# Two re-placings in a hybrid attention layer: one value chunk's casts, and the post norm's half sums

## The chip, the cores and the metric

The kernel runs on one core of one Trainium2 chip. The metric is the device time of one execution in microseconds (us); smaller is better. The engines are called as the profile calls them: PE (TensorE) multiplies matrices, PEld is its weight load, DVE (VectorE) and ACT (ScalarE) do elementwise work, POOL (GpSimd) and SP (SyncE) issue DMAs. Each engine takes its own instructions strictly in the order in which they stand in its queue.

## The reference, cut to what matters

One layer over 512 latent tokens of width 1024 (x) and 256 context tokens (ctx), in float32:

```python
sh, sc, gt = _modulation(c, w_mod, b_mod)                 # gt: the gain of the post norm
h  = _rmsnorm(x, pre_g) * (1 + sc) + sh                   # hc alike from ctx
parts = _split_in(h @ w_in)                               # ten parts of 1024 columns
q, k, v = rope(heads(parts[4])), rope(heads(parts[5])), heads(parts[6])
k_c, v_c = split(hc @ w_in[:, K_OFF:V_END])
attn = _neighbourhood_attention(q, k, v, k_c, v_c, rpb)   # one softmax over window and context
y_a = (silu(z_a) * b_gate * dwconv3(c_gate * x_in)) @ w_out_conv
y_b = (silu(z_b) * attn) @ w_out_attn
y = (sigmoid(g_a) * y_a + sigmoid(g_b) * y_b) @ w_o
x = x + gt * _rmsnorm(y, post_g)
```

The change touches two pieces of this: the projection to v (and v_c) for the second group of heads, and the 1024 values of `gt`, which are a matrix-vector product of silu(c) with a third of `w_mod`.

## The kernel before, in words

Every float32 operand of a matmul is split into a rounded part H and a rest L (`split`, L66 to 76): ACT casts H (L68), DVE subtracts it (L71), and three matmuls (H·H, H·L, L·H) stand for one.

**Weights** come in chunks of 256 columns, each as four loads of 256 KB into a ring of six slots (`Chunk`, L97, on SP's queue). A plain chunk (`split`, L100) makes two casts of 128x4x256 and two subtractions of the same shape. A paired chunk (`first`, `second`) makes sums of its quarters in place in the ring (L112 to 129) and casts of 128x512, and `pair` (L304 to 327) then needs seven products (L299) in place of eight; between them ACT and DVE combine the partial sums (L310, L313, L315, L321 on ACT, L316, L324, L327 on DVE). The list `order` (L246 to 250) says in which order chunks come, and `paired` (L243) which are paired. `Chunks.load` issues the loads of the next chunk; in the attention stage the chunk's casts (`ready`) are put into the list `behind`, which is run at the end of the score block (L875).

**The attention stage** runs 64 score blocks (8 pairs of heads, 2 heads, 4 blocks of 128 tokens), written two blocks ahead. A block's bias comes by L715; its scores are L723 or L732 on PE, L739 on DVE (bias and row maximum), L746 or L750 on ACT (exponential with sum). After two blocks follow the reciprocal (L751, DVE), the scaling (L753, ACT), eight transposes (L760, PE) and the split of the result into TH (L68) and TL (L71); after four the gather L779. Into these blocks `plan` (L228) puts projection work: `keys_queries` (queries and keys of a pair; L206 and L211 project the context's keys, L217 and L218 add two halves, L628 and L629 rotate) and `values(g)` (L187 and L192 for each of six groups of tokens, g being a group of two pairs of heads). The place of this case is the end of `keys_queries(2)` and the start of `values(1)`, whose chunk is the first plain value chunk in the attention stage.

**The merge stage** (L967 to 1003) runs j = 0 to 7. Each j has two units (i = 0, 1) of 24 matmuls (L174 to 176), each followed by a gate update on DVE (L973), and the sum m of the two (L980). For j < 4 it also projects the gates of j + 4 by `merge_gates` (a `pair` with 7 x 12 matmuls L299). The new gate tile G[j + 4] lies in the buffer of G[j], so the first copy into it, L310, waits for L980 of the same j.

**The post norm's gains** are computed beside it: `gain_half` (L955) fetches half a row block of `w_mod` (128x512, 256 KB, L959, tile `wg`, three buffers) and reduces it against silu(c) on DVE (L960). Sixteen halves make the gains; L986 to 988 finish them, L995 copies and L996 transposes them in j = 4.

The order within an engine is the program's order only in part: a scheduler moves an instruction ahead where it expects it to be ready, unless `tc.keep_in_program_order` holds the instruction in its place on its engine. In the kernel before the scheduler puts all sixteen halves into j = 0 and j = 1, though the program has four in each j from 0 to 3.

Of the kernel before, what the change touches and what calls it, by code (L numbers as in the profile page):

```python
# [9 lines left out]
F32 = mybir.dt.float32  # L10
F32R = mybir.dt.float32r
AF = mybir.ActivationFunctionType
ALU = mybir.AluOpType
AX = mybir.AxisListType

P = 128
D = 1024
KT = 8
S = 512
# [4 lines left out]
PG, QG, BM, CW, CB = 0, 8, 16, 40, 64  # L24
# [3 lines left out]
def layer(ctx: ExitStack, tc, xp, ctxt, ctxT, cc, wmod, small, wfirst, win, wout, wo, rel, tab, out):  # L28
    nc = tc.nc
# [4 lines left out]
    cv = ctx.enter_context(tc.tile_pool(name="cv", bufs=2))  # L34
# [13 lines left out]
    sp = const.tile([P, 72], F32, name="sp")  # L48
# [5 lines left out]
    gains = const.tile([P, KT], F32, name="gains")  # L54
# [33 lines left out]
    class Chunk:  # L88
# [8 lines left out]
                    nc.sync.dma_start(ring[:, at + o], src[:, 2 * i + o])  # L97
                self.raws.append(ring[:, at:at + 2].rearrange("p u (k c) -> p u k c", k=4))

        def split(self):  # L100
            t = [wtile([P, 4, 2, 256]) for _ in range(2)]
            for x, raw in zip(t, self.raws):
                H, L = (x[:, :, y].rearrange("p k (u c) -> p k u c", u=2) for y in range(2))
                split(H, L, raw.rearrange("p u k c -> p k u c"))
            k = range(KT)
            return tuple([t[i // 4][:, i % 4, y] for i in k] for y in range(2)) + ([t[i // 4][:, i % 4] for i in k],)

# [28 lines left out]
    behind = None  # L136

    class Chunks:
# [5 lines left out]
        def load(self, n):  # L144
            if n < len(self.srcs) and n not in self.ahead and n not in self.raw:
                self.raw[n] = Chunk(self.srcs[n][0])
                if behind is None:
                    self.ready(n)
                else:
                    behind.append(lambda: self.ready(n))  # L150

        def ready(self, n):
            if n in self.raw:
                c, kind = self.raw.pop(n), self.srcs[n][1]
                self.ahead[n] = c.first(kind == "qk") if kind else c.split()

        def __call__(self):
            self.load(self.n)
# [82 lines left out]
        "cx": lambda j: win[2 * j], "bz": lambda j: win[2 * j + 1],  # L241
    }
    def paired(n, i):  # L243
        return n == "g" or n == "qk" and i in (2, 3, 4, 6) or n == "zb" and i < 3 or n in ("cx", "bz") and i > 3

    order = [(win[i], False) for i in range(8)] + [(qk(0), False), (vz(0, 0), False)]  # L246
    order += [(where[n](i), n if paired(n, i) else False) for f in plan for n, i in f] + [(vz(3, 1), paired("zb", 3))]
# [138 lines left out]
    with ExitStack() as p0:  # L386
# [17 lines left out]
        cols = {}  # L404
# [435 lines left out]
    for p in range(NPAIR):  # L840
        f = []
# [8 lines left out]
    blocks = [(p, h, b) for p in range(NPAIR) for h in range(2) for b in range(4)]  # L850
    pts = {n: scores(*blocks[n]) for n in range(2)}
    T = None
    behind = []
    done = 0
    for i, (p, h, b) in enumerate(blocks):
        slot = i % 8
        if slot == 0:
            items = chain(*(g for g, _ in fill[p]))
            total, done = sum(n for _, n in fill[p]), 0
        upto = -(-total * (slot + 1) // 8)  # L860
        while done < upto:
            step(items)
            done += 1
        if T is not None and b == 0:
            gather(*T)
        if i + 2 < len(blocks):
            pts[i + 2] = scores(*blocks[i + 2])
        if b == 0:
            TH = aw.tile([P, 4, 4, P], F32R, name="TH", bufs=1)
            TL = aw.tile([P, 4, 4, P], F32R, name="TL", bufs=1)  # L870
            T = p, h, TH, TL

        if b % 2:
            turn2([pts.pop(i - 1), pts.pop(i)], b - 1, TH, TL)
        for f in behind:  # L875
            f()
        behind = []
    behind = None
    last = gate2(3)
    next(last)  # L880
# [72 lines left out]
    cond = bp.tile([P, D], F32, name="cond", tag="gpost")  # L953
    nc.sync.dma_start(cond, csc.broadcast_to([P, D]))

    def gain_half(k, i):
        t = cv.tile([P, S], F32, name="wg", tag="tc", bufs=3)
        cols = slice(i * S, (i + 1) * S)
        nc.sync.dma_start(t, wmod[16 + k][:, cols])  # L959
        nc.vector.tensor_tensor_reduce(  # L960
            out=t, in0=t, in1=cond[:, cols], scale=1.0,
            scalar=sp[:, BM + 16 + k:BM + 17 + k] if i == 0 else bsc1[:, k:k + 1],
            op0=ALU.mult, op1=ALU.add, accum_out=(bsc1 if i == 0 else gains)[:, k:k + 1],
        )

    for j in range(KT):
        w = chunk()  # L967
        g = [G[j][:, i] for i in range(2)]
        if j in (4, 6):
            raws[j // 2] = G[j]  # L970
        m2 = raws[j // 2][:, j % 2]
        for i in range(2):
            nc.vector.scalar_tensor_tensor(  # L973
                out=g[i], in0=g[i], scalar=1.0, in1=unit(w, i, ua[i]), op0=ALU.add, op1=ALU.mult
            )
            if j == 7 and i == 0:
                A2 = [bp.tile([P, 2, S], F32R, name=f"A2{k}", tag=f"us{k}") for k in range(4)]
                for k in range(3):
                    split(A2[k][:, 0], A2[k][:, 1], raws[2 + k // 2][:, k % 2])
        nc.vector.tensor_add(m2, g[0], g[1])  # L980
        if j < 4:
            for n, _ in enumerate(merge_gates(j + 4)):
                for i in range(2):
                    gain_half(2 * j + n, i)
        if j == 4:
            nc.vector.tensor_mul(gains, gains, sp[:, QG:QG + KT])  # L986
            nc.vector.tensor_scalar(out=gains[:, 0:4], in0=gains[:, 0:4], scalar1=0.5, scalar2=None, op0=ALU.mult)
            nc.vector.tensor_scalar(out=gains[:, 4:8], in0=gains[:, 4:8], scalar1=-0.5, scalar2=None, op0=ALU.mult)
            gpost = bp.tile([P, D], F32, name="gpost", tag="gpost")
            for i in range(2):  # L990
                gb = cv.tile([P, S], F32, name="ta")
                ps = pj()
                for k in range(4):
                    n = 4 * i + k
                    nc.vector.tensor_copy(gb[:, k * P:(k + 1) * P], gains[:, n:n + 1].broadcast_to([P, P]))  # L995
                    nc.tensor.transpose(ps[:, k * P:(k + 1) * P], gb[:, k * P:(k + 1) * P], ident)  # L996
                nc.scalar.copy(gpost[:, i * S:(i + 1) * S], ps)
        if j == 4:
            A11, S3 = operand("A11", hp, ("u2", "u3")), operand("S3", hp, ("a2", "a3"))
            for q in range(2):  # L1000
                split(A11[q][:, 0], A11[q][:, 1], raws[q][:, :, h0])
                x = cv.tile([P, S], F32, name="tb").rearrange("p (k c) -> p k c", k=2)
                nc.vector.tensor_sub(x, raws[q][:, :, h0], raws[q][:, :, h1])
                split(S3[q][:, 0], S3[q][:, 1], x)
            B11, B12 = quarter("B11", hp, ("s0", "s1")), quarter("B12", hp, ("u0", "u1"))
            B22, B21, T2, T3 = (quarter(n, hp, (f"h{2 * i}", f"h{2 * i + 1}")) for i, n in enumerate(("B22", "B21", "T2", "T3")))
            for t, i in ((B11, (0, 0)), (B12, (0, 1)), (B22, (1, 1)), (B21, (1, 0))):
                load_block(t, *i)
        if j == 5:
            sums1(0)  # L1010
        if j == 6:
            nc.scalar.activation(const.tile([P, 1], F32, name="dummy2"), G[7][:, 1, :1], AF.Sqrt, bias=eps, scale=0.0)
            wB11 = moving(B11)
            total(B11, B11, B12)
            T1 = B11
            total(T2, T1, B22)
            total(T3, B12, B22)
            T4 = B12
            total(T4, T2, B21)
# [208 lines left out]
```

## Time and profile before

| | us |
|---|---|
| median of 3 runs (lowest, highest) | 706.83 (706.29, 706.86) |
| the profiled execution's own time | 707.08 |
| its span, first to last instruction | 705.3 |
| PE busy | 692.5 (98%) |
| DVE busy | 603.1 (86%) |
| ACT busy | 444.4 (63%) |
| granted TensorE clock, mean | 0.999 |

The profile is one execution; its own time is 0.25 us over the median, and 1.8 us of it lie outside the span. A timeline row gives start, duration, engine, line, operation, tiles (out<-in) and how many instructions are drawn together; in brackets stands how long the engine was idle before and what released it. Instructions overlap in their engine's pipeline, so the step from one start to the next is shorter than a duration. PE's ends are modelled, so that its idle time is read best from starts.

### The profile page before, as it was taken

How to read it: one execution, taken by the hardware profiler on the slowest of the kernel's cores; microseconds unless marked ns; L12 is line 12 of the kernel's file. 1: busy time of each engine (PE TensorE's matmuls, PEld its weight loads, DVE VectorE, ACT ScalarE, POOL GpSimd, SP SyncE). 2: the span in 40 equal slices, each digit the busy share in tenths (PEclk: the TensorE clock that was granted, in tenths of full speed). 3: DMA queues.
4: the chain of work that ended last, by engine and by line, in shares of the span. 5: the costliest groups of instructions: out<-in, count | busy, mean ns of one | idle time of the engine just before them, and what ended most of it. 6: DMA issues, size and time to landing. Idle time of an engine off the chain costs nothing.

```text
span 705.3 us, 11954 instructions
## 1 busy us (share of the span) xinstructions
PE 692.5 (98%) x4304; PEld 621.6 (88%) x4304; DVE 603.1 (86%) x1170; ACT 444.4 (63%) x895; POOL 66.7 (9%) x110
## 2 busy tenths in 40 slices
PE   7999999999999999999999999999999999999996
PEld 5888888889979999898999989999898889988885
DVE  7999998669897999878998797999799896665996
ACT  7668543558677687675875757788683434442563
POOL 0000003131040310402103113000000000000000
PEclk9999999999999999999999999999999999999999
DMA  8996845454352473453635436334464643660013
GB/s 353 406 346 197 307 167 134 111 113 131 120 135 75 117 192 121 106 149 77 169 119 128 118 104 158 100 117 138 146 216 158 201 145 111 202 246 31 31 60 120
DMA packets 51727, 108.84 MB, mean 154 GB/s; under 512 B 6610, under 2 KB 6866, under 8 KB 51668
## 3 DMA queue, kind: packets, MB, share of 16 engines
q1 hardware_dynamic: 43202, 92.73, 38.6%
q0 software_dynamic: 8320, 15.21, 11.0%
q8 instruction: 34, 0.56, 0.3%
q14 instruction: 25, 0.20, 0.1%
q10 hardware_dynamic: 146, 0.14, 0.1%
HBM read 87.60 MB, written 5.25 MB: 132 GB/s over the span
## 4 chain that ended last, share of the span: by engine, by line
PE 79%; DVE 11%; DMA 6%; ACT 3%; issue 2%; SPq 0%; ACTq 0%; POOL 0%; DVEq 0%
PE ps L299 23%; PE ps L174 8%; PE ps L176 8%; PE ps L175 8%; PE ps L187 6%; PE ps L1026 5%; DVE w L71 4%; PE ps L779 3%; PE ps L192 3%; PE ps L760 3%; DMA ring<-in_win 3%; PE ps L723 3%; PE ps L457 2%; PE ps L463 2%; PE ps L460 2%; PE ps L206 2%
## 5 line engine op out<-in xcount | busy, mean ns | idle before, releaser
L71 DVE TENSOR_TENSOR w<-ring,w 128x512 fp32r<-128x512 f32 (+1 forms) x209 | 163.1, 796 | 31.8 <-ACT w L68 30.9
L68 ACT CAST w<-ring 128x512 fp32r<-128x512 f32 (+1 forms) x209 | 142.1, 711 | 76.5 <-PE ps L176 20.9
L299 PE MATMUL ps<-S,w 128*128 128x256 f32 x1104 | 140.6, 283 | 1.4 <-ACT g L310 1.4
L299 PEld LDWEIGHTS ps<-S,w 128*128 128x128 f32 x1104 | 135.9, 192 | 1.9 <-ACT g L310 1.6
L299 PE MATMUL ps<-h,w 128*128 128x256 f32 x828 | 108.0, 284 | 0.0
L299 PEld LDWEIGHTS ps<-h,w 128*128 128x128 f32 x828 | 103.3, 191 | 2.2 <-DVE g L316 0.2
L174 PE MATMUL ps<-h,w 128*128 128x512 f32 x160 | 62.6, 391 | 0.0
L175 PE MATMUL ps<-h,w 128*128 128x512 f32 x160 | 62.5, 390 | 0.0
L176 PE MATMUL ps<-h,w 128*128 128x512 f32 x160 | 62.1, 389 | 0.0
L631 POOL DMA_DIRECT2D tc<-tb x32 | 28.6, 1048 | 291.5 <-DVE tc L629 173.1
L753 ACT ACTIVATE pt<-pt,z 128x512 f32<-128x512 f32 x64 | 43.0, 723 | 7.7 <-DVE z L751 7.6
L71 DVE TENSOR_TENSOR TL<-ps,TH 128x512 fp32r<-128x512 f32 x64 | 42.5, 681 | 0.7 <-ACT TH L68 0.3
L68 ACT CAST TH<-ps 128x512 fp32r<-128x512 f32 x64 | 35.8, 587 | 10.9 <-PE ps L760 10.9
L739 DVE CUSTOM_DVE_ANT_1 ps<-ps,bt 128x512 f32<-128x512 f32 x56 | 38.7, 691 | 4.2 <-PE ps L723 4.1
L176 PEld LDWEIGHTS ps<-h,w 128*128 128x128 f32 x160 | 30.0, 188 | 6.4
L175 PEld LDWEIGHTS ps<-h,w 128*128 128x128 f32 x160 | 30.1, 188 | 6.2
L174 PEld LDWEIGHTS ps<-h,w 128*128 128x128 f32 x160 | 30.0, 188 | 6.1
L760 PE MATMUL ps<-ident,pt 128*128 128x128 f32 x256 | 33.4, 273 | 0.6 <-ACT pt L753 0.6
L187 PE MATMUL ps<-w,h 128*128 128x512 f32 x128 | 32.3, 394 | 0.0
L760 PEld LDWEIGHTS ps<-ident,pt 128*128 128x128 f32 x256 | 29.2, 140 | 3.0 <-ACT pt L753 1.2
L746 ACT ACTIVATE pt<-ps,m 128x512 f32<-128x512 f32 x32 | 22.1, 689 | 14.6 <-DVE m L739 14.1
L779 PE MATMUL ps<-TH,V 128*128 128x256 f32 (+1 forms) x96 | 28.4, 318 | 0.0
(251 smaller groups left out, 1393.2 us busy)
## 6 DMA issues: line engine op xcount, KB each, us to landing
ring<-in_win SPq DMA_DIRECT2D x148, 256.0 KB, 3.4
wm<-in_wmod SPq DMA_DIRECT2D x26, 512.0 KB, 7.5
ring<-in_wout SPq DMA_DIRECT2D x32, 256.0 KB, 3.6
bt<-in_rel SPq DMA_DIRECT2D x16, 256.0 KB, 2.9
tc<-tb POOLq DMA_DIRECT2D x32, 128.0 KB, 2.9
wg<-in_wmod SPq DMA_DIRECT2D x16, 256.0 KB, 3.7
B<-in_wo SPq DMA_DIRECT2D x8, 512.0 KB, 6.5
fraw<-in_wfirst SPq DMA_DIRECT2D x8, 384.0 KB, 8.4
```

The lines of the kernel that those rows point to most:

```text
L68: cast = nc.scalar.copy(H, src)
L71: nc.vector.tensor_sub(L, src, H.bitcast(F32))
L174: nc.tensor.matmul(ps, lhsT=H[k][:, cs], rhs=mH[k], start=k == 0, stop=False)
L175: nc.tensor.matmul(ps, lhsT=H[k][:, cs], rhs=mL[k], start=False, stop=False)
L176: nc.tensor.matmul(ps, lhsT=L[k][:, cs], rhs=mH[k], start=False, stop=k == KT - 1)
L187: nc.tensor.matmul(ps, lhsT=mH[k][:, ts], rhs=both[k].rearrange("p a c -> p (a c)"), start=k == 0, stop=False, skip_group_check=True,)
L299: nc.tensor.matmul(ps, lhsT=w[:, x, k], rhs=act[y][k], start=start and k + o == 0, stop=k == 3 and o == 2, skip_group_check=True,)
L739: nc.vector.tensor_tensor_reduce(out=s3, in0=s3, in1=bt[:, e::4 - e][:, 0:2], scale=-1.0, scalar=3.0e38, op0=ALU.add, op1=ALU.min, accum_o ...
L753: nc.scalar.mul(x, x, z[:, i:i + 1])
L760: nc.tensor.transpose(tp[:, c], pt[:, c * P:(c + 1) * P], ident)
L779: nc.tensor.matmul(o3[:, dst], lhsT=V[p][:, kt, h], rhs=src(t), start=n == 0 and t is TH, stop=n == len(work) - 1 and t is TL,)
L1026: nc.tensor.matmul(out, lhsT=a(x, k, ts), rhs=w[y][k // 2][:, k % 2, cols], start=start and k + o == 0, stop=k == 3 and o == 2, skip_group ...
```

## The change

Two edits. In the first, `paired` marks the value chunk ("v", 1) with the kind "v". It is still split as a plain chunk, but its two casts are held in program order on ACT, and `behind` is now two lists, so that this chunk's casts are written one score block later than others'. In the second, the fetch of a half is a function of its own: three are fetched ahead of the loop, and each reduction is followed by the fetch three further on. The reductions are held in program order on DVE, one after each gate update and one after each of the two units of `merge_gates`, so four in each j from 0 to 3.

```diff
-        def split(self):
+        def split(self, pinned=False):
...
-                split(H, L, raw.rearrange("p u k c -> p k u c"))
+                split(H, L, raw.rearrange("p u k c -> p k u c"), pinned=pinned)
...
-                    behind.append(lambda: self.ready(n))
+                    behind[self.srcs[n][1] == "v"].append(lambda: self.ready(n))
...
-                self.ahead[n] = c.first(kind == "qk") if kind else c.split()
+                self.ahead[n] = c.first(kind == "qk") if kind and kind != "v" else c.split(kind == "v")
...
-        return n == "g" or n == "qk" and i in (2, 3, 4, 6) or n == "zb" and i < 3 or n in ("cx", "bz") and i > 3
+        return n == "g" or n == "v" and i == 1 or n == "qk" and i in (2, 3, 4, 6) or n == "zb" and i < 3 or n in ("cx", "bz") and i > 3
...
-    behind = []
+    behind = [], []
...
-        for f in behind:
+        for f in behind[0]:
             f()
-        behind = []
+        behind = [behind[1], []]
...
-    def gain_half(k, i):
-        t = cv.tile([P, S], F32, name="wg", tag="tc", bufs=3)
-        cols = slice(i * S, (i + 1) * S)
-        nc.sync.dma_start(t, wmod[16 + k][:, cols])
-        nc.vector.tensor_tensor_reduce(
+    halves, fetched = [(k, slice(i * S, (i + 1) * S)) for k in range(KT) for i in range(2)], []
+
+    def fetch_half():
+        if len(fetched) < len(halves):
+            k, cols = halves[len(fetched)]
+            t = cv.tile([P, S], F32, name="wg", tag="tc", bufs=3)
+            nc.sync.dma_start(t, wmod[16 + k][:, cols])
+            fetched.append(t)
...
+    def gain_half():
+        n = turned[0]
+        turned[0] += 1
+        (k, cols), t = halves[n], fetched[n]
+        tc.keep_in_program_order(nc.vector.tensor_tensor_reduce(
             out=t, in0=t, in1=cond[:, cols], scale=1.0,
...
+        ))
+        fetch_half()
+
+    for _ in range(3):
+        fetch_half()
...
+            if j < 4:
+                gain_half()
...
         nc.vector.tensor_add(m2, g[0], g[1])
         if j < 4:
-            for n, _ in enumerate(merge_gates(j + 4)):
-                for i in range(2):
-                    gain_half(2 * j + n, i)
+            for _ in merge_gates(j + 4):
+                gain_half()
```

Below the first edit, lines keep their numbers up to L955; behind it L959 becomes L962, L960 becomes L971, L973 becomes L988, L980 becomes L997, L986 to 988 become L1002 to 1004, L995 and L996 become L1011 and L1012, L1003 becomes L1019.

The order of ACT's queue around the value chunk, before. The chunk's two casts are w_1995 and w_1996; tc_1907 (L321) belongs to the keys of pair 2, ps_1985 and ps_2046 are two score blocks, and TH_1993 takes the transposes of the two blocks ahead of these.

```order
L68 CAST w_1896<-ring_105 128x512
L68 CAST w_1995<-ring_105 128x4x256
L784 COPY ta_1981<-ps_1968 64x512
L68 CAST w_1996<-ring_105 128x4x256
L746 ACTIVATE pt_1990,z_1991<-ps_1985,m_1988 128x512
L321 COPY tc_1907<-ps_1909 128x256
L68 CAST w_2235<-ring_105 128x512 x2
L68 CAST TH_1993<-ps_2058 128x512
L68 CAST TH_1993<-ps_2059 128x512
L750 ACTIVATE pt_2053,z_1991<-ps_2046,m_2051 128x512
L753 ACTIVATE pt_1990<-pt_1990,z_1991 128x512
L753 ACTIVATE pt_2053<-pt_2053,z_1991 128x512
```

The same stretch of the changed kernel, where the chunk's casts are w_2066 and w_2067:

```order
L68 CAST w_1896<-ring_105 128x512
L784 COPY ta_1981<-ps_1968 64x512
L746 ACTIVATE pt_1990,z_1991<-ps_1985,m_1988 128x512
L321 COPY tc_1907<-ps_1909 128x256
L68 CAST TH_1993<-ps_2052 128x512
L68 CAST TH_1993<-ps_2053 128x512
L68 CAST w_2066<-ring_105 128x4x256
L750 ACTIVATE pt_2047,z_1991<-ps_2040,m_2045 128x512
L68 CAST w_2067<-ring_105 128x4x256
L217 COPY ta_2101<-ps_2084 128x256
L753 ACTIVATE pt_1990<-pt_1990,z_1991 128x512
L753 ACTIVATE pt_2047<-pt_2047,z_1991 128x512
```

The exponential L746, the copy L321 and the TH casts now stand ahead of both casts of the chunk, and the first casts of the chunk after it (w_2235) have left this stretch.

PE's queue a little later in the same stage, as a difference: L760 are the transposes of the next two score blocks, L187 the first matmuls of `values(1)`.

```order
 L723 MATMUL ps<-ks,qd 128x512
 L723 MATMUL ps<-ks,qe 128x512
-L760 MATMUL ps<-ident,pt 128x128 x8
 L187 MATMUL ps<-w,h_82 128x512
 L187 MATMUL ps<-w,h_83 128x512
 L187 MATMUL ps<-w,h_84 128x512
+L760 MATMUL ps<-ident,pt 128x128 x8
 L187 MATMUL ps<-w,h_85 128x512
 L187 MATMUL ps<-w,h_86 128x512
```

Three matmuls of the value projection now stand ahead of those transposes.

DVE's queue in j = 1 of the merge stage, before: from the first half behind the first gate update to the sum m (L980) and the half behind it. Each ISA row with an input is one half's reduction, the row below it the reading of its result; g1 is the gate tile, w_6592 and w_6593 are operands of the gates of j = 5.

```order
L960 ISA wg_7061,bsc1_115<-wg_7061,cond_6320,sp_72 128x512
L960 ISA bsc1_115 128x1
L960 ISA wg_7108,bsc1_115<-wg_7108,cond_6320,sp_72 128x512
L960 ISA bsc1_115 128x1
L71 TENSOR_TENSOR w_6592<-ring_105,w_6592 128x512 x2
L960 ISA wg_7064,gains_81<-wg_7064,cond_6320,bsc1_115 128x512
L960 ISA gains_81 128x1
L973 SCALAR_TENSOR_TENSOR g1_5756<-g1_5756,ps_6564 128x512
L71 TENSOR_TENSOR w_6593<-ring_105,w_6593 128x512
L980 TENSOR_TENSOR m0_6318<-g1_5756 128x512
L960 ISA wg_7111,gains_81<-wg_7111,cond_6320,bsc1_115 128x512
```

And in the changed kernel, from the first gate update of j = 1:

```order
L988 SCALAR_TENSOR_TENSOR g1_5756<-g1_5756,ps_6544 128x512
L971 ISA wg_6402,bsc1_115<-wg_6402,cond_6320,sp_72 128x512
L971 ISA bsc1_115 128x1
L71 TENSOR_TENSOR w_6604<-ring_105,w_6604 128x512 x2
L988 SCALAR_TENSOR_TENSOR g1_5756<-g1_5756,ps_6573 128x512
L971 ISA wg_6480,gains_81<-wg_6480,cond_6320,bsc1_115 128x512
L971 ISA gains_81 128x1
L997 TENSOR_TENSOR m0_6318<-g1_5756 128x512
L71 TENSOR_TENSOR w_6605<-ring_105,w_6605 128x512
L1019 TENSOR_TENSOR tb_7209<-m0_6318 128x512
L316 TENSOR_TENSOR g5_6603<-g5_6603,ps_6613 128x256
```

Between the two gate updates one half stands where three stood, and one stands between the second update and the sum m, where none stood. L316, on DVE, needs the copy L310 and stands behind m in both kernels.

More of the change, by code (lines that the diff above doesn't have):

```diff
@@ L954, in layer @@
     nc.sync.dma_start(cond, csc.broadcast_to([P, D]))
-    def gain_half(k, i):
-        t = cv.tile([P, S], F32, name="wg", tag="tc", bufs=3)
-        cols = slice(i * S, (i + 1) * S)
-        nc.sync.dma_start(t, wmod[16 + k][:, cols])
-        nc.vector.tensor_tensor_reduce(
-            out=t, in0=t, in1=cond[:, cols], scale=1.0,
-            scalar=sp[:, BM + 16 + k:BM + 17 + k] if i == 0 else bsc1[:, k:k + 1],
-            op0=ALU.mult, op1=ALU.add, accum_out=(bsc1 if i == 0 else gains)[:, k:k + 1],
-        )
+    halves, fetched = [(k, slice(i * S, (i + 1) * S)) for k in range(KT) for i in range(2)], []
[5 more added lines that the diff above has]
+            fetched.append(t)
+    turned = [0]
+    def gain_half():
[3 more added lines that the diff above has]
+        tc.keep_in_program_order(nc.vector.tensor_tensor_reduce(
+            out=t, in0=t, in1=cond[:, cols], scale=1.0,
+            scalar=bsc1[:, k:k + 1] if n % 2 else sp[:, BM + 16 + k:BM + 17 + k],
+            op0=ALU.mult, op1=ALU.add, accum_out=(gains if n % 2 else bsc1)[:, k:k + 1],
+        ))
+        fetch_half()
+    for _ in range(3):
+        fetch_half()
     for j in range(KT):
```

## The prediction

> **What bounds the kernel now.** I read what PE waited for first, since PE is busy for 98% of the span. Its longest waits in the whole run (line; total us, times, longest):
>
> ```profile
> PE ps L507 <- ACT crow L479: 3.7, 1, 3.7
> PE ps L299 <- ACT g L310: 1.4, 1, 1.4
> PE ps L206 <- ACT tc L321: 0.7, 1, 0.7
> PE ps L760 <- ACT pt L753: 0.6, 1, 0.6
> ```
>
> The first is the start-up, which the change doesn't touch. The second lies in the merge stage, the third and fourth in the value stage, and these are the change's two places. The table by stage (length; busy us of PE, PEld, DVE, ACT, POOL; clock) shows both places and stretches without a wait:
>
> ```profile
> 188.00:204.00 16.00, 14.76 (x98) 12.85 (x97) 13.51 (x30) 11.32 (x26) 3.53 (x4) 1.00 0.55 154
> 204.00:222.00 18.00, 18.00 (x110) 15.98 (x109) 13.66 (x36) 12.09 (x32) 4.66 (x9) 1.00 0.47 113
> 240.00:266.00 26.00, 26.00 (x210) 25.39 (x209) 25.77 (x55) 21.64 (x48) 7.38 (x13) 1.00 0.69 176
> 552.00:573.00 21.00, 19.56 (x120) 17.47 (x119) 18.81 (x47) 7.51 (x12) 0.00 (x0) 1.00 0.53 177
> 573.00:594.00 21.00, 21.00 (x135) 19.10 (x134) 13.61 (x21) 8.57 (x14) 0.00 (x0) 1.00 0.37 121
> ```
>
> In rows 1 and 4 PE is idle; in the others it is busy for the whole stretch. So nearly the whole kernel is a queue of matmuls, and time saved in rows 1 and 4 reaches the end if no later stretch takes it back. PE's starts tell how long each wait is. First an undisturbed group of transposes:
>
> ```profile
> 173.15 1.03 PE L760 MATMUL ps<-ident,pt 128*128 128x128 f32 x8
> 173.94 1.31 PE L299 MATMUL ps<-h,w 128*128 128x256 f32 x9
> ```
>
> Eight of them take 0.79 from start to next start. In the value stage:
>
> ```profile
> 193.04 1.03 PE L760 MATMUL ps<-ident,pt 128*128 128x128 f32 x8
> 194.75 2.11 PE L206 MATMUL ps<-hc,w 128*128 128x512 f32 x8 [0.67 <-ACT tc L321]
> ...
> 198.11 0.39 PE L723 MATMUL ps<-ks,qd 128*128 128x512 f32 x1
> 198.34 0.40 PE L723 MATMUL ps<-ks,qe 128*128 128x512 f32 x1
> 199.31 1.27 PE L760 MATMUL ps<-ident,pt 128*128 128x128 f32 x8 [0.57 <-ACT pt L753]
> 200.34 2.09 PE L187 MATMUL ps<-w,h 128*128 128x512 f32 x8
> ```
>
> L206 could start at 193.04 + 0.79 = 193.83 and starts 0.92 later. The step from one L723 to the next is 0.23, so the last should hand over at 198.57, and L760 starts 0.74 later. L187 follows after 1.03 in place of 0.79, as the second four transposes wait too: 0.24. The place loses 0.92 + 0.74 + 0.24 = 1.90.
>
> Why it waits is in ACT's rows and in the chain that ended last:
>
> ```profile
> 192.71 1.05 ACT L68 CAST w<-ring 128x1024 fp32r<-128x1024 f32 x1 [3.34 <-DMA ring<-in_win]
> 193.67 0.68 ACT L746 ACTIVATE pt<-ps,m 128x512 f32<-128x512 f32 x1
> 194.24 0.19 ACT L746 ACTIVATION_READ_ACCUMULATOR pt<-ps,m 128x1 f32 x1
> 194.33 0.36 ACT L321 COPY tc<-ps 128x256 f32<-128x256 f32 x1
> 194.59 1.15 ACT L68 CAST w<-ring 128x512 fp32r<-128x512 f32 x2
> 195.63 1.08 ACT L68 CAST TH<-ps 128x512 fp32r<-128x512 f32 x2
> 196.71 0.69 ACT L750 ACTIVATE pt<-ps,m 128x512 f32<-128x512 f32 x1
> 197.30 0.19 ACT L750 ACTIVATION_READ_ACCUMULATOR pt<-ps,m 128x1 f32 x1
> 198.53 1.33 ACT L753 ACTIVATE pt<-pt,z 128x512 f32<-128x512 f32 x2 [1.04 <-DVE z L751]
> ```
>
> ```profile
> 188.72 3.97 DMA ring<-in_win
> ```
>
> The ring load issued at 188.72 lands at 192.69. ACT stands for 3.34 in front of the chunk's second cast, with L746 and L321, which need nothing of it, queued behind. PE then waits for L321, and later for L753, whose exponentials came late by the same stand.
>
> In the merge stage:
>
> ```profile
> 565.79 1.60 PE L299 MATMUL ps<-S,w 128*128 128x256 f32 x12
> 568.83 1.70 PE L299 MATMUL ps<-S,w 128*128 128x256 f32 x12 [1.44 <-ACT g L310]
> 570.36 1.60 PE L299 MATMUL ps<-h,w 128*128 128x256 f32 x12
> 571.80 0.40 PE L299 MATMUL ps<-S,w 128*128 128x256 f32 x2
> ```
>
> Twelve such matmuls take 571.80 - 570.36 = 1.44. The second row should start at 565.79 + 1.44 = 567.23 and starts 1.60 later; its own twelve take 1.53, 0.09 more. The place loses 1.69. The copy L310 is released by the sum m:
>
> ```profile
> 565.76 0.74 DVE L960 CUSTOM_DVE_ANT_0 wg<-wg,cond,bsc 128x512 f32<-128x512 f32 x1
> ...
> 566.43 0.68 DVE L973 SCALAR_TENSOR_TENSOR g<-g,ps 128x512 f32<-128x512 f32 x1
> 567.03 0.68 DVE L71 TENSOR_TENSOR w<-ring,w 128x512 fp32r<-128x512 f32 x1
> 567.63 0.68 DVE L980 TENSOR_TENSOR m<-g 128x512 f32<-128x512 f32 x1
> ```
>
> ```profile
> 568.40 0.37 ACT L310 COPY g<-ps 128x256 f32<-128x256 f32 x1 [4.54 <-DVE m L980]
> ```
>
> The matmuls that feed this L973 are over at about 563: between them and the row of 565.79 stand twenty-four L299, twice 1.44. The update comes 3.4 later, behind halves and casts on DVE.
>
> **The change part by part.**
>
> *The value chunk, later and pinned.* The casts go behind L746, L321 and both TH casts, so the landing at 192.69 holds up none of these. L321 then stands behind L746 alone. Without the 3.34 it ends at 194.33 + 0.36 - 3.34 = 191.4, well ahead of 193.83, so the 0.92 goes whole. Behind the transposes, from about 193.65 on, ACT's new order has two TH casts (1.08), a cast (steps of 0.96, from 192.71 to 193.67), L750 (0.59 to 0.69), the second cast (0.96) and L217 (0.35, as L321 with the same shape), together about 3.9: free at 197.55. z, behind the chunk's first subtraction on DVE, is ready by about 197.1, so L753 runs from 197.55 at 0.66 each to 198.87. PE, 0.92 earlier, ends its L723 at 197.65, fills 0.7 with the three L187 moved ahead (at L723's step), and comes to L760 at 198.34. Its second four wait until 198.9 in place of 198.7: about 0.2 of the 1.90 stays. Gain 1.7. Its bounds: 1.9 if L753 is in time, and 0.9 if the pinned casts hold up L753 as much as the late load did before.
>
> What is moved past: the three L187 need the chunk's first subtraction, which I put at 197.0, 0.6 ahead of them; that cover is the thinnest here, and each tenth beyond it costs a tenth. The next chunk's ring loads wait for these subtractions, so its casts move from 194.6 to about 201 by my replay. They stand on ACT then, with its 18.00 - 12.09 = 5.9 us of room from 204 to 222. SP now issues a score block's bias load (L715) ahead of four ring loads; by my replay L723 of the block held up longest still has 3 us. DVE takes about 2 us of subtractions later, against 18.00 - 13.66 = 4.3 us of room in the same row. Cost nothing, if that room serves; from 240 to 266 DVE has 0.23 left in 26, so what isn't caught up by then comes out as PE time.
>
> *The halves, four in each j.* In j = 1 the second gate update no longer has halves queued before it: the row at 565.76, and two more ahead of it. Its result is there at 563.1; update, one half (a step of 0.67, from 565.76 to 566.43) and m (0.6) end at about 565.1, and L310 ends at 565.45, 1.8 ahead of PE's 567.23. So the wait goes whole: gain 1.7, bounds 1.5 (a start alone, without the slower twelve) and 1.8 (a like but smaller delay in j = 0). The eight halves that move to j = 2 and 3 cost DVE 4 x 0.67 = 2.7 in each; the last row of the table leaves it 21.00 - 13.61 = 7.4. There the second update is followed by one half in place of a cast's subtraction (0.60), which moves behind m, so L310 stays within 0.1 of its place. The final gains come some 50 us later, and their transposes in j = 4 keep about 3 us by the same replay. Cost nothing, under that cover.
>
> *The fetches.* They are as many as before; three go out ahead of the loop, each further one waits on SP for the half three before it. A ring load behind one is late by at most a step of 0.67. In the new order a fetch and its use lie at least 8 us apart, by the rows of PE between them. Landing times before (least, median, most):
>
> ```profile
> DMA to landing us min/median/max: 2.5/3.7/5.2
> ```
>
> ```profile
> DVE wg L960 <- DMA wg<-in_wmod: 2.9, 3, 2.2
> ```
>
> The waits of the second row, 2.9 in all, are DVE's and go; they are not added, as PE's wait holds what they cost.
>
> The sum: 1.7 + 1.7 = 3.4. Against the profiled execution's own 707.08 that is 703.7; this execution lies 0.25 over the median, 706.83, and on the median it is 703.4.
>
> PE's idle time in the table gives less: 16.00 - 14.76 + 21.00 - 19.56 = 2.7, so 704.1. By weight loads, 12.85 in 16 against a share of 15.98/18 is 1.5 us short, and 17.47 in 21 against 19.10/21 is 1.8 short: 3.3, or 703.5. The Trainium skill ("Perfetto Trace Analysis", Identifying the Most-Contended Engine) calls matmul busy time a poor measure, since matmuls overlap, and weight-load busy time a good one; by that page it would be 703.5 rather than 704.1, and the starts here side with it.
>
> **The rivals.**
>
> *Only one gain arrives.* In the value stage, a late z or a late subtraction in front of the moved L187, or DVE being still behind at 240, gives the 1.7 back: 706.8 - 1.7 = 705.1. For it speaks the 0.23 of room in row 3, against it the 4.3 ahead of that. Or the merge gain is lost, because another operand (a cast of L71 behind the pinned half) is late in L310's place: 705.1 again. Against it stands the 1.8 of slack.
>
> *The change doesn't do what it says.* The scheduler's new order might leave ACT as it was; but the printed orders show both moves. That leaves PE's waits being replaced in full at both places: 706.8.
>
> *Slower: the pinned halves wait for their fetches.* A half held on DVE stands ahead of m, and everything behind it stands with it, m, L310 and PE. Before, the scheduler could set a late half behind other work, and even so DVE waited three times, up to 2.2. From a wait of 1.8 on it reaches PE. If the fetch ahead fails (a fetch held up on SP behind ring loads that wait for slots) and each j from 0 to 3 waits for one whole landing at the median, that is 4 x (3.7 - 1.8) = 7.6 on top of 703.4: 711.0. It comes out slower than before by over 0.2% once the waits add 4.8 to PE, so at 3.0 in each of the four. Against it is the lead of 8 us, over the longest landing of 5.2. The Trainium skill ("DMA: Bandwidth & Descriptors", Anatomy of one DMA) has about 2.0 us and a byte term, for another DMA path; estimated from that page, 256 KB take 2.6, and this rival would cost 3.2 in place of 7.6 and end at 706.6. The landing row above, with 3.7 at its median, disagrees with it.
>
> **How the numbers follow.** Both gains 0.68, at 703.1 to 704.4 by the bounds (1.9 + 1.8 at best, 0.9 + 1.5 at worst); the runs before reach 0.54 under their median, so 702.6 to 704.4. One alone 0.20, at 704.9 to 705.3. Nothing 0.05, at 706.8. Slower 0.07, up to 711.0. The range takes in the first two cases: 702.6 to 705.3. About 0.2%, or 1.4 us, can be told from no change here, so faster means below 705.4: the first case and most of the second, 0.84; same 0.09; slower 0.07.
>
> **What would show it.** Right: no wait of PE for L321 and none over 0.3 for L753 near 190 to 200; L206 0.79 behind the transposes; ACT not idle for a ring load before L321; L310 in j = 1 done by 566 on this profile's scale, without a PE wait; four halves in each j, with no DVE wait for a fetch; the rows from 204 and 573 on as full of PE as before. Wrong: a new PE wait for w or z at the moved L187 or L760; a PE wait between 204 and 270 that was not there; DVE waiting for wg in front of m; a PE wait for L310 in j = 2 or 3.

## The result, and the profile after

The changed kernel takes 703.97 us (median of 8 runs, 703.29 to 704.94) beside 706.66 before (8 runs, 705.10 to 707.95). The ratio is 0.9964, with a 95% interval of 0.9952 to 0.9975: faster by 2.5 us, from 1.8 to 3.4. The forecast was 703.4 in a range from 702.6 to 705.3, with faster at 0.84.

The profiled execution after took 703.79, with a span of 702.0, against 707.08 and 705.3 before: 3.29 less. PE's waits, in the same view as before (line; total us, times, longest):

```profile
PE ps L507 <- ACT crow L479: 3.7, 1, 3.7
PE ps L457 <- ACT h L555: 0.4, 1, 0.4
PE ps L779 <- DVE TL L71: 0.3, 1, 0.3
```

The three waits that the prediction named are gone, and one is new: L779 for TL. The table by stage, with the rows that answer to those of before:

```profile
188.00:204.00 16.00, 16.00 (x109) 14.46 (x108) 12.03 (x26) 10.28 (x21) 4.62 (x6) 1.00 0.57 150
204.00:222.00 18.00, 17.74 (x111) 15.62 (x110) 15.74 (x44) 14.44 (x40) 3.58 (x7) 1.00 0.47 108
240.00:266.00 26.00, 26.00 (x210) 25.39 (x209) 25.77 (x56) 21.25 (x47) 6.39 (x11) 1.00 0.67 171
552.00:573.00 21.00, 21.00 (x133) 19.09 (x132) 16.27 (x30) 8.61 (x15) 0.00 (x0) 1.00 0.46 150
573.00:594.00 21.00, 21.00 (x134) 19.10 (x133) 15.77 (x29) 8.62 (x15) 0.00 (x0) 1.00 0.47 152
```

PE (first number behind the length) is now full in the first and fourth rows, which had 1.24 and 1.44 us of idle time; the second row has lost 0.26, and the third is as full as it was. DVE's load in the fourth fell from 18.81 to 16.27 and rose in the fifth from 13.61 to 15.77, as the halves moved.

The value stage, on PE:

```profile
193.01 1.04 PE L760 MATMUL ps<-ident,pt 128*128 128x128 f32 x8
193.80 2.08 PE L206 MATMUL ps<-hc,w 128*128 128x512 f32 x8
...
197.60 0.85 PE L187 MATMUL ps<-w,h 128*128 128x512 f32 x3
198.29 1.20 PE L760 MATMUL ps<-ident,pt 128*128 128x128 f32 x8
199.25 1.40 PE L187 MATMUL ps<-w,h 128*128 128x512 f32 x5
```

and on ACT:

```profile
191.29 0.37 ACT L321 COPY tc<-ps 128x256 f32<-128x256 f32 x1 [1.29 <-PE ps L299]
193.64 1.08 ACT L68 CAST TH<-ps 128x512 fp32r<-128x512 f32 x2 [1.98 <-PE ps L760]
194.60 1.06 ACT L68 CAST w<-ring 128x1024 fp32r<-128x1024 f32 x1
...
197.42 1.36 ACT L753 ACTIVATE pt<-pt,z 128x512 f32<-128x512 f32 x2
```

L321 waits for PE alone and ends at 191.66. L206 starts 0.79 behind the transposes, with no wait. L187 follows L760 after 0.96 in place of 0.79: of the second wait 0.17 is left. ACT no longer waits for a ring load here.

The merge stage, j = 1, on DVE, ACT and PE:

```profile
561.52 0.69 DVE L988 SCALAR_TENSOR_TENSOR g<-g,ps 128x512 f32<-128x512 f32 x1 [0.45 <-PE ps L176]
562.12 0.74 DVE L971 CUSTOM_DVE_ANT_0 wg<-wg,cond,bsc 128x512 f32<-128x512 f32 x1
562.80 0.08 DVE L971 DVE_READ_ACCUMULATOR2_ANT gains<- 128x1 f32 x1
562.80 0.68 DVE L997 TENSOR_TENSOR m<-g 128x512 f32<-128x512 f32 x1
```

```profile
563.57 0.37 ACT L310 COPY g<-ps 128x256 f32<-128x256 f32 x1 [1.38 <-DVE m L997]
```

```profile
564.19 3.04 PE L299 MATMUL ps<-S,w 128*128 128x256 f32 x24
567.07 1.60 PE L299 MATMUL ps<-h,w 128*128 128x256 f32 x12
```

The second gate update now waits for PE, not for halves; L310 ends at 563.94, and PE runs its twenty-four matmuls in 2.88 without a break (567.07 - 564.19).

The new wait is behind the value stage. PE, ACT, DVE and the transfer there:

```profile
204.23 0.39 PE L779 MATMUL ps<-TH,V 128*128 128x512 f32 x1
204.88 0.50 PE L779 MATMUL ps<-TL,V 128*128 128x512 f32 x1 [0.26 <-DVE TL L71]
205.22 0.40 PE L779 MATMUL ps<-TH,V 128*128 128x512 f32 x1
```

```profile
200.55 0.58 ACT L73 ACTIVATE qd<-tc 128x448 fp32r<-128x448 f32 x1 [1.77 <-DMA tc<-tb]
201.04 0.57 ACT L68 CAST TH<-ps 128x512 fp32r<-128x512 f32 x1
201.50 0.41 ACT L68 CAST ks<-ta 128x256 fp32r<-128x256 f32 x1
201.81 0.59 ACT L68 CAST TH<-ps 128x512 fp32r<-128x512 f32 x1
```

```profile
201.94 0.42 DVE L71 TENSOR_TENSOR kl<-ta,ks 128x256 fp32r<-128x256 f32 x1 [1.87 <-ACT ks L68]
203.54 1.28 DVE L71 TENSOR_TENSOR TL<-ps,TH 128x512 fp32r<-128x512 f32 x2
```

```profile
195.25 5.22 DMA tc<-tb
```

ACT stands 1.77 us in front of L73, a cast of pair 2's queries, which needs their rotation (L631, a DMA on POOL's queue that took 5.22 to land). The two TH casts and the ks cast stand behind L73. DVE then stands 1.87 in front of kl, which needs the ks cast, and kl and two L739 stand ahead of the two TL (201.94 to 203.54). So TL comes late, and PE waits for it. In the kernel before, L73 stood behind these casts and waited for nothing:

```profile
201.84 0.60 ACT L68 CAST TH<-ps 128x512 fp32r<-128x512 f32 x1
202.32 0.71 ACT L750 ACTIVATE pt<-ps,m 128x512 f32<-128x512 f32 x1
202.99 0.74 ACT L73 ACTIVATE qd<-tc 128x448 fp32r<-128x448 f32 x2
```

In the changed kernel's PE rows the step from 204.23 to 205.22 is 0.99 in place of two steps of 0.235: 0.52 lost.

PE's starts, matmul by matmul, give the whole account. The table has the lead of the changed kernel over the one before at each matmul, from both traces:

| place (us, before) | lead there, us | change |
|---|---|---|
| up to 193 | 0.03 | |
| L206, 194.75 | 0.95 | +0.92 |
| value projection, 201.35 | 1.78 | +0.83 |
| L779, 206.48 | 1.26 | -0.52 |
| L723, 221.10 | 1.19 | -0.07 |
| L299 in the gates made ahead of the loop, 526.72 | 1.49 | +0.30 |
| L299 in j = 0, 546.38 | 1.61 | +0.12 |
| L299 in j = 1, 569.05, and to the end | 3.30 | +1.69 |

### The profile page after: what moved, and what is told of

The parts are those of the page before. It is cut to its first block, busy times and chain, and to the rows that moved or that the text cites. A ratio compares the mean times of both kernels' runs of the same rounds, so it can differ in the third digit from the quotient of the medians.

```text
span 702.0 us, 11959 instructions
## 1 busy us (share of the span) xinstructions
PE 691.8 (99%) x4304; PEld 621.7 (89%) x4304; DVE 603.9 (86%) x1170; ACT 444.7 (63%) x895; POOL 66.7 (10%) x110
## 4 chain that ended last, share of the span: by engine, by line
PE 95%; DVE 2%; ACT 1%; DMA 1%; issue 0%; POOL 0%; ACTq 0%; DVEq 0%
PE ps L299 33%; PE ps L174 9%; PE ps L176 9%; PE ps L175 9%; PE ps L187 6%; PE ps L1042 5%; PE ps L779 4%; PE ps L760 4%; PE ps L723 3%; PE ps L192 3%; PE ps L206 2%; PE ps L457 2%; PE ps L463 2%; PE ps L460 2%; PE ps L732 1%; PE ps L211 1%
## 5 line engine op out<-in xcount | busy, mean ns | idle before, releaser
L71 DVE TENSOR_TENSOR w<-ring,w 128x512 fp32r<-128x512 f32 (+1 forms) x209 | 163.0, 796 | 31.2 <-ACT w L68 29.6
L299 PE MATMUL ps<-S,w 128*128 128x256 f32 x1104 | 140.2, 283 | 0.0
L299 PEld LDWEIGHTS ps<-S,w 128*128 128x128 f32 x1104 | 135.8, 192 | 0.2 <-ACT tc L310 0.2
L299 PE MATMUL ps<-h,w 128*128 128x256 f32 x828 | 107.9, 284 | 0.0
L299 PEld LDWEIGHTS ps<-h,w 128*128 128x128 f32 x828 | 103.4, 191 | 1.8
L631 POOL DMA_DIRECT2D tc<-tb x32 | 28.6, 1048 | 287.2 <-DVE tc L629 206.7
L753 ACT ACTIVATE pt<-pt,z 128x512 f32<-128x512 f32 x64 | 43.0, 723 | 6.9 <-DVE z L751 6.8
L71 DVE TENSOR_TENSOR TL<-ps,TH 128x512 fp32r<-128x512 f32 x64 | 42.3, 681 | 0.7 <-ACT TH L68 0.3
L739 DVE CUSTOM_DVE_ANT_1 ps<-ps,bt 128x512 f32<-128x512 f32 x56 | 38.7, 692 | 4.4 <-PE ps L723 4.3
L760 PE MATMUL ps<-ident,pt 128*128 128x128 f32 x256 | 33.3, 273 | 0.0
L187 PE MATMUL ps<-w,h 128*128 128x512 f32 x128 | 32.4, 394 | 0.0
L760 PEld LDWEIGHTS ps<-ident,pt 128*128 128x128 f32 x256 | 29.2, 140 | 2.2 <-ACT pt L753 0.4
L746 ACT ACTIVATE pt<-ps,m 128x512 f32<-128x512 f32 x32 | 22.1, 689 | 13.5 <-DVE m L739 12.8
L779 PE MATMUL ps<-TH,V 128*128 128x256 f32 (+1 forms) x96 | 28.4, 318 | 0.0
```

The lines of the kernel that those rows point to most:

```text
L71: nc.vector.tensor_sub(L, src, H.bitcast(F32))
L187: nc.tensor.matmul(ps, lhsT=mH[k][:, ts], rhs=both[k].rearrange("p a c -> p (a c)"), start=k == 0, stop=False, skip_group_check=True,)
L299: nc.tensor.matmul(ps, lhsT=w[:, x, k], rhs=act[y][k], start=start and k + o == 0, stop=k == 3 and o == 2, skip_group_check=True,)
L739: nc.vector.tensor_tensor_reduce(out=s3, in0=s3, in1=bt[:, e::4 - e][:, 0:2], scale=-1.0, scalar=3.0e38, op0=ALU.add, op1=ALU.min, accum_o ...
L753: nc.scalar.mul(x, x, z[:, i:i + 1])
L760: nc.tensor.transpose(tp[:, c], pt[:, c * P:(c + 1) * P], ident)
```

## The experiments

My theory after this: the value edit is worth about 1.75 at its place and gives back what L73 costs at L779; the merge edit is worth 1.8; the 0.30 near 526 comes from a ring load that landed 1.3 us sooner and is chance. The rivals are named with each run. The runs of one batch share one chip and the runs of the kernel before: 707.13 (16 runs) for the first four, 706.50 (15 runs) for the next four, 706.56 (23 runs) for the last three.

**both_again** is the changed kernel, without an edit.

> The changed kernel once more, unchanged. Theory: the profile of the changed kernel gained 1.75 us in the value stage, lost 0.52 again to one new wait (PE's L779 on TL) and 0.07 more, and gained 1.8 in the merge stage; another 0.3 near 526 us came from a ring load that landed 1.3 us sooner and is chance. So 703.7 to 704.2 against about 706.7, and a profile with the L779 wait again and an offset near 526 between 0 and 0.3. Rival A: the L779 wait is chance too, from the one rotation DMA that took 5.2 us to land; then it is absent here, and the time is about 703.3.

Measured 704.03, ratio 0.9954 (0.9939 to 0.9970). The profile has no wait at L779, and the 0.30 near 526 again, though the order there is that of before.

**v_only** has the value edit alone; `gain_half` and its calls are those of the kernel before.

> Only the value chunk's casts are moved and held; the half sums are as before. Theory: the two edits add, and this one is worth 1.2 us net (1.75 less the new wait at L779): 705.5. Rival B: the stage behind it takes back what the value stage gains, because DVE and ACT are late there: 706.5. Rival A (the L779 wait is chance): 705.0.

Measured 705.59, ratio 0.9978 (0.9964 to 0.9992), 1.5 us under before. Its value stage gains 1.74 on PE, and L779 takes back 0.28. Its merge stage, in the order of before, loses less than before did:

```profile
565.01 1.60 PE L299 MATMUL ps<-S,w 128*128 128x256 f32 x12
567.42 1.70 PE L299 MATMUL ps<-S,w 128*128 128x256 f32 x12 [0.81 <-ACT g L310]
```

567.42 - 565.01 - 1.44 is 0.97, and with the slower twelve 1.07, where the first profile lost 1.69.

**m_only** has the merge edit alone.

> Only the half sums are spread and held; the value chunk is as before. Theory: 1.7 at the one PE wait for L310 and 0.1 at a smaller one: 704.9. Rival: the merge gain was in part lent by the earlier stages, so that alone it brings under 1: 706. No DVE wait for wg in front of the sum m under either.

Measured 705.54, ratio 0.9978 (0.9966 to 0.9991), 1.6 us under before. The merge stage gains 1.69 and 0.12 on PE, as in the changed kernel, and no half waits for its fetch. The sum of the two single edits, 1.5 + 1.6 = 3.1, is what both bring in the same batch (707.13 - 704.03). Within their intervals, each about 2 us wide, they add, and neither single edit is told apart from the other in size. This profile has the value stage in the order of before: it loses 1.7 there.

**th_first** holds L73 of pair 2, and the first cast of the chunk behind the value chunk, in program order on ACT.

```diff
-            nc.scalar.mul(H, src, scale)
+            (tc.keep_in_program_order if pinned else id)(nc.scalar.mul(H, src, scale))
...
-                split(qd[0][:, dst], qe[0][:, dst], q[:, src], 0.125)
+                split(qd[0][:, dst], qe[0][:, dst], q[:, src], 0.125, pinned=p == 2)
...
-            split(t[:, 0, 0], t[:, 0, 1], b11)
+            split(t[:, 0, 0], t[:, 0, 1], b11, pinned=pinned)
...
-                self.ahead[n] = c.first(kind == "qk") if kind and kind != "v" else c.split(kind == "v")
+                self.ahead[n] = c.first(kind == "qk", n == 15) if kind and kind != "v" else c.split(kind == "v")
```

> The changed kernel, and on ACT the two casts L73 of pair 2's queries and the first cast of the chunk behind the value chunk are held in program order, which puts the two TH casts and the ks cast ahead of them. Theory: ACT's 1.8 us stand on L73, which waited for the rotation DMA, made DVE's TL and PE's L779 late; without it the wait at L779 goes and 0.5 us come on top of the changed kernel: 703.2 to 703.5, with the value stage's full 1.7. Rival A: the wait was chance, and this is the same as the changed kernel. Rival C: another operand of L779 or the later queries (L723 of pair 2) are late in their place: 704 or more.

Measured 703.86, ratio 0.9951 (0.9937 to 0.9964): not to be told from both_again. ACT and PE:

```profile
199.43 1.19 ACT L68 CAST TH<-ps 128x512 fp32r<-128x512 f32 x2
200.52 0.41 ACT L68 CAST ks<-ta 128x256 fp32r<-128x256 f32 x1
201.41 0.72 ACT L73 ACTIVATE qd<-tc 128x448 fp32r<-128x448 f32 x2 [0.49 <-DMA tc<-tb]
```

```profile
204.74 0.40 PE L779 MATMUL ps<-TH,V 128*128 128x512 f32 x1
204.97 0.40 PE L779 MATMUL ps<-TL,V 128*128 128x512 f32 x1
205.21 0.39 PE L779 MATMUL ps<-TH,V 128*128 128x512 f32 x1
```

The rotation's landings reached 5.6 us here, more than in the changed kernel's first profile, and L779 does not wait: nothing that it needs stands behind L73 any longer.

**v_nodelay** keeps the hold but writes the casts at their old block.

```diff
-                    behind[self.srcs[n][1] == "v"].append(lambda: self.ready(n))
+                    behind[0].append(lambda: self.ready(n))
```

> The changed kernel, but the value chunk's two casts, still held in program order, are written at the block at which they were before, so that they stand behind L746 and ahead of L321 and the TH casts. Theory: what counts is which instructions stand behind the casts when the ring load lands; L321 then ends at about 194.0 on the scale of before in place of 191.7, PE loses 0.3 there, and L753 is about as late as in the changed kernel or by up to 0.7 more: 704.3 to 705.0. Rival: the hold alone does it, and the later block nothing: 704.0, with no PE wait for L321. Other rival: it is as bad as before the change: 705.5.

Measured 704.46, ratio 0.9960 (0.9946 to 0.9974). On ACT:

```profile
193.06 1.05 ACT L68 CAST w<-ring 128x1024 fp32r<-128x1024 f32 x1 [1.31 <-DMA ring<-in_win]
194.01 0.36 ACT L321 COPY tc<-ps 128x256 f32<-128x256 f32 x1
```

The whole execution lies 0.8 later than before's up to here, so this L321 is 1.1 us earlier than before's 194.33, and L206 waits for nothing (0.79 behind its transposes). Not all of the 1.1 is the order: 0.7 is the step of L746 (193.67 to 194.33 in the profile before), behind which the held casts now stand, and 0.4 is a ring load that landed sooner (193.06 - 0.8 is 192.3, where before's second cast started at 192.71). With the landing of before, the hold alone would take an estimated 0.7 of the 0.92 away. L753 is late: PE waits 0.8 for it. On PE the place gains 0.7 in place of 1.75, so the second wait needs the later block.

**m_late** writes and holds each fetch right ahead of its reduction, with none ahead of it in the program.

```diff
-            nc.sync.dma_start(t, wmod[16 + k][:, cols])
+            tc.keep_in_program_order(nc.sync.dma_start(t, wmod[16 + k][:, cols]))
...
+        fetch_half()
         (k, cols), t = halves[n], fetched[n]
...
-        fetch_half()
-
-    for _ in range(3):
-        fetch_half()
```

> The changed kernel, but each half's fetch is written and held on SP right ahead of its reduction, with none fetched ahead. Theory: SP is free to issue as soon as one of the three buffers is, so the fetches still lead by several us unless they stand behind ring loads that wait for a slot; a few DVE waits for wg of under 1.5 us, none of which reaches PE: 704.0 to 704.5. Rival (the slower case of the prediction): fetches are late by a landing of 3 to 4 us in front of the sum m in several j, PE waits for L310 each time: 706 to 711.

Measured 703.83, ratio 0.9957 (0.9944 to 0.9969). No half waits for its fetch. Landing times there (least, median, most):

```profile
DMA to landing us min/median/max: 3.5/4.0/5.4
```

The fetches are slow enough to matter, but SP runs ahead of DVE by itself, as far as the three buffers let it: in this trace each fetch goes out at least 8.4 us before its reduction starts. Fetching three ahead is not what brings the gain; the place of the reductions on DVE is.

**m_front3** puts three of a j's halves ahead of m and holds m behind them.

```diff
-            if j < 4:
+            for _ in range(3 * i if j < 4 else 0):
                 gain_half()
...
-        nc.vector.tensor_add(m2, g[0], g[1])
+        (tc.keep_in_program_order if j < 4 else id)(nc.vector.tensor_add(m2, g[0], g[1]))
...
-            for _ in merge_gates(j + 4):
-                gain_half()
+            for n, _ in enumerate(merge_gates(j + 4)):
+                n and gain_half()
```

> The changed kernel, but three of a j's four halves stand between the second gate update and the sum m, and the sum is held behind them; the fourth follows after the second unit of the gates. Fetches still lead. Theory: m comes 1.3 us later, up to 1.9 with the casts that stay between, against a slack of 1.7 before L310 holds up PE: PE loses 0 to 0.3 in each of four j, 704.0 to 705.2. Rival: L310 is not what limits there, and nothing changes: 704.0 and no PE wait for L310. Other rival: the slack is far smaller than 1.7: over 706.

Measured 704.64, ratio 0.9966 (0.9954 to 0.9979), 0.7 over the changed kernel's first 703.97 in the medians, though the intervals overlap. In j = 1, on PE and ACT:

```profile
564.23 1.60 PE L299 MATMUL ps<-S,w 128*128 128x256 f32 x12
565.93 1.70 PE L299 MATMUL ps<-S,w 128*128 128x256 f32 x12
```

```profile
565.50 0.37 ACT L310 COPY g<-ps 128x256 f32<-128x256 f32 x1
```

Against the changed kernel, L310 is 1.9 later by its distance from the first twelve (565.50 - 564.23 = 1.27, against 563.57 - 564.19 = -0.62), and PE starts the second twelve 0.26 late (565.93 - 564.23 - 1.44). The slack is 1.9 - 0.26 = 1.6. Start by start against the changed kernel, the four j together cost PE 0.5.

**m_front4** puts all four ahead of the held m (4 in place of 3 above, and none in `merge_gates`).

> As with three, but all four halves of a j stand ahead of the held sum m, so that the fourth has to wait for a fetch that is issued only when the first is done. Theory: 2.0 us for three more halves, and a DVE wait of 0.5 to 1.7 for the fourth fetch, against a slack of 1.7: PE waits 0.8 to 2.0 for L310 in each of four j, 707 to 712, which is the prediction's slower case made on purpose. Rival: the fetch is there in time: 705 to 706, and no DVE wait for wg.

Measured 706.96 (11 runs), ratio 1.0006 (0.9996 to 1.0016): the whole gain of both edits is lost. Waits for L310 and for a fetch in j = 3:

```profile
DVE wg L971 <- DMA wg<-in_wmod: 1.6, 1, 1.6
PE ps L299 <- ACT g L310: 1.2, 1, 1.2
```

In j = 0 to 2 the second twelve come 4.56 behind the first (548.17 against 543.61 in j = 0) in place of 1.44, but the scheduler had filled that time with matmuls of the next unit: start by start against the changed kernel, each of these j loses 0.4, and j = 3 loses 1.9. The time is just under the 707 to 712 that I expected, and the mechanism is only in part the one that I named: one fetch is late, in j = 3, and in the others a subtraction of an operand that waits for ACT stands ahead of the fourth half.

**before_again** is the kernel before, for a second profile.

> The kernel before, unchanged, for a second profile. Theory: its losses are waits for transfers, so their sizes are drawn anew in each execution: the value stage loses 1.4 to 1.9 again (a ring load of 3.4 to 4 us), the merge stage 0.6 to 1.7 at L310 (the execution of the kernel with the value edit alone lost only 1.1 there, with the same order), and the 0.3 near 526 us of the first profile is gone. Rival: the merge loss is 1.7 each time, as the first profile has it.

Measured 706.93, ratio 0.9997 (0.9985 to 1.0009). Two of its waits on PE:

```profile
PE ps L299 <- ACT g L310: 2.5, 1, 2.5
PE ps L760 <- ACT pt L753: 0.6, 1, 0.6
```

The ring load landed a microsecond sooner (the second cast starts at 191.74 in place of 192.71): it went out 0.81 sooner, at 187.91, and took 0.16 less. So the wait for L321 is gone, with no edit, and the value stage loses 1.0 in place of 1.9. The merge stage loses 2.75 in place of 1.69. DVE stood longer for one fetch, in the profile before and here:

```profile
555.10 0.75 DVE L960 CUSTOM_DVE_ANT_0 wg<-wg,cond,bsc 128x512 f32<-128x512 f32 x1 [2.16 <-DMA wg<-in_wmod]
```

```profile
554.80 0.75 DVE L960 CUSTOM_DVE_ANT_0 wg<-wg,cond,bsc 128x512 f32<-128x512 f32 x1 [3.03 <-DMA wg<-in_wmod]
```

From this half to the sum m DVE works without a break, and L310 starts 13.3 us behind it, in both and in v_only (553.69 to 567.00). So the late half sets when L310 comes, and PE loses what it is early by. Here PE reaches the first twelve 1.35 sooner than in the profile before (564.44 against 565.79), the half only 0.30 sooner, and the loss grows by 1.05; in v_only PE is 0.78 sooner and the half 1.41, and the loss shrinks by 0.63. Whether fetching ahead alone, with the halves left in the old order, would take this wait away was not run. The rival, 1.7 each time, falls; my own bounds of 0.6 to 1.7 and 1.4 to 1.9 were too narrow as well. The 0.30 near 526 is there without any edit, as in every profile but one: it was the first profile of before that was late there.

**both_third** and **th_first_again** are the changed kernel and th_first once more, side by side.

> The changed kernel a third time, beside the next kernel. Theory: 703.9 to 704.2, with a profile in which PE loses 0.3 to 0.7 at L779 in two executions of three, by how late the rotation DMA lands.

> The kernel with the TH casts held ahead of L73 a second time. Theory: no PE wait at L779 whatever the landing, and 0.3 to 0.4 us under the changed kernel in the mean: 703.6 to 703.8. Rival: no difference that can be told.

Measured 704.33 (12 runs), ratio 0.9971 (0.9960 to 0.9981), with 0.66 lost at L779; and 703.33 (5 runs), ratio 0.9957 (0.9945 to 0.9969), with nothing lost there. The intervals overlap. In both batches th_first is the lower one, by 0.2 and 1.0, which fits the 0.3 to 0.5 expected and doesn't prove it; its 703.33 is the lowest median of all the runs here.

What L779 lost, over all profiles with the value edit whole:

| kernel | ACT's stand on L73 ahead of the TH casts, us | lost at L779, us |
|---|---|---|
| both_again | 1.21 | 0.00 |
| m_front3 | 1.26 | 0.02 |
| v_only | 1.52 | 0.28 |
| changed kernel | 1.77 | 0.52 |
| m_late, both_third | 1.91, 1.91 | 0.66, 0.66 |
| m_front4 | 2.02 | 0.77 |
| th_first, th_first_again | none ahead of TH | 0, 0 |

In these profiles each tenth of a stand above about 1.25 costs a tenth. Rival A, that the wait is chance, is right about its size in one execution and wrong about its cause.

## Why the prediction was right, point by point

- **The value place, 1.7.** Measured 1.75 up to the end of its first group, against the first profile of before. The 0.92 at L206 went whole; the second L760 kept 0.17 where I had put 0.2. L187 in front of L760 did not wait: the subtraction that it needs ended at 197.25, 0.35 ahead of it, where I had put 0.6. But 0.92 was the size of one execution: in before_again the wait for L321 was not there, with the old order.
- **"Cost nothing, if that room serves".** This step failed. Over 204 to 222 there was room on ACT and DVE, but not at the right place in the queue: I followed the casts of the next chunk and the subtractions past each other, and did not follow L73 and the POOL queue's rotation behind it. In the kernel before, L73 stood behind both TH casts and L750; in the new order it stands ahead of all three. It cost 0.52 in the first profile and 0 to 0.77 in others. Against the 1.90 of the first profile of before the edit is thus worth 1.0 to 1.75; against the 1.0 of before_again it would be 0.1 to 0.85. By the runs of v_only it is 1.5, in an interval from 0.6 to 2.5.
- **The merge place, 1.7.** Measured 1.69, and 0.12 in j = 0. That the wait goes whole was right. But the sum took the size of a wait from one execution as if it were fixed: the same order lost 1.07 and 2.75 there in two others, by when one fetch landed against PE's own time.
- **Slack of 1.8 before L310 holds up PE.** Measured 1.6.
- **The covers of the merge stage.** Right: four halves in each j, no half that waits for its fetch, no PE wait for L310 in j = 2 or 3. The one DVE wait that the profile puts down to a fetch, 0.6 at 586.50, is in front of a cast's subtraction (L71), which reads no half, and PE does not wait there.
- **The fetches.** Their lead over the reductions is at least 11.97 us in the trace, where I had put at least 8, and was more than was needed; m_late has none fetched ahead and is no slower.
- **The slower rival.** Not seen in the changed kernel. With m held behind four halves (m_front4) the gain goes, but no more: 707, where I had priced the rival at 711. The price had a whole landing in each of four j; there only j = 3 waited for a fetch, 1.6, and in j = 0 to 2 PE had other matmuls for most of the time in which I had let it stand idle. A late fetch in every j was never run, so the price of that stays untested.
- **The sum.** 3.4 against 3.3 in the profiles and 2.7 in the medians (interval 1.8 to 3.4). The agreement of the profiles is partly luck: 0.30 near 526 that no edit brought stands against 0.59 given back, and the old order lost 1.0, 1.7 and 1.9 in the value stage and 1.07, 1.69 and 2.75 in the merge stage, by execution. The estimate from weight loads gave 3.3, that from PE's idle time 2.7; by starts the two places came to 1.75 and 1.69. The Trainium skill ("Perfetto Trace Analysis", Identifying the Most-Contended Engine) calls matmul busy time a poor measure of how close a kernel is to roofline and points to weight-load busy time; at these two places the estimate from weight loads was the closer one.

## What to carry to other kernels

A wait on an in-order engine costs what stands behind it, so a late operand is best moved behind all that doesn't need it; but then read which instruction stands first in its place, and what that one waits for. Take the size of a wait for a transfer from several executions: the order says where it can occur, the landing says how much. And when an edit has a hold, a delay and a fetch ahead in one, try each by itself. Here the hold alone brought 0.7 of the 1.75 at the value place, part of it by a load that landed sooner, and the later block the rest; in the merge stage the place of the reductions brought the gain, and the fetch ahead nothing.

## What the runs showed of the hardware

The rotation's DMAs of this place (128 KB each, on POOL's queue) landed in 2.6 to 2.9 us in the kernel before and in m_only. No ring load ran beside them there: in the profile before the first goes out at 198.72, and the last ring load had landed at 198.56. A bias load still ran beside the first one, until 199.65. In the nine profiles with the value edit whole they go out about 4 us sooner, in the changed kernel's first profile beside the bias load at 195.00 and four ring loads from 197.27 on, and the slowest landing of each profile is 4.7 to 5.6. The Trainium skill ("DMA: Bandwidth & Descriptors", Queues, rings and completion order) says that each DMA engine takes turns between the queues that have work. The longer landings agree with that, though no run here kept the new order and took the loads away from beside them, so the cause of the longer landing stays open.

The kernel before took 705.2 to 708.8 in 23 runs of one batch. Two waits for transfers lie in PE's path there, and both changed in size from profile to profile, as told above. A third source lies outside the change: PE's first wait, for L479, was 3.7 us in some profiles and 4.1 to 4.3 in others. How much of the spread each of them makes was not measured.
